# Two products per token row, one core: 25-token tiles with split stores become 15-token tiles with one store each

## The chip, the core and the metric

The kernel runs on one core of one Trainium2 chip. The metric is the device time of one execution in microseconds (us); lower is better. Before the change it is 239.96 us, the median of three runs (239.96 to 240.86). One further execution was recorded by the profiler: it took 239.6 us, of which 237.8 us lie between its first and its last instruction (the span). A difference of about 0.5%, 1.2 us, is the least that a measurement of this kernel can tell from no change.

## What is computed

```python
def reference(x, expert_indices, expert_weights):
    batch, seq, hidden = x.shape            # 16, 1024, 512
    k = expert_indices.shape[-1]            # 2
    x_expanded = x[:, :, np.newaxis, :].repeat(k, axis=2)
    weights = expert_weights[..., np.newaxis]
    return (x_expanded * weights).astype(np.float32)
```

There are 16,384 tokens of 512 numbers in fp32. Every token row is multiplied by its two weights, and both products are written. The indices are not used. So 33.6 MB of x and 0.13 MB of weights are read, 67.1 MB are written, and there are 16.8 million multiplications: hardly any arithmetic for the bytes.

## The kernel before, in words

The 16,384 tokens stand on 128 partitions, 128 tokens to a partition. They are cut into five tiles of 25 tokens per partition (L32) and a rest of 3 (`LAST`, L34, `z_tile`). One token of x is 2 KB on a partition, its two products are 4 KB, so that a tile is 50 KB in and 100 KB out on each partition. In a transfer of 128 partitions each of the 16 DMA engines moves 8 rows; a row is one contiguous piece and shows in the profile as one packet.

**Loads** (`load`, L67 to L85) are issued by ScalarE's queue (ACT). Tile 0 comes in two parts of 9 and 16 tokens (`FIRST`, L35), each later tile in one. Two tiles of x fit (`bufs=2`, L43), so `load(i + 2)` stands behind the work on tile i (L159) and must wait until that work has read the buffer. The loads of tiles 0 and 1 and of `z_tile` stand at the beginning.

**Weights** (`weights`, L92 to L105) are three transfers on SyncE's queue (SP), issued between the two parts of load 0: 25 KB for tile 0, 100 KB for tiles 1 to 4, 3 KB for the rest. Their rows are 200 bytes and 24 bytes long.

**Products** go to `o_ring` (L47), one buffer as large as a whole tile's output. `emit` (L148) cuts a tile into pieces of 13 and 12 tokens (tiles 0 and 1) or 9, 8 and 8 (tiles 2 to 4, L157). In each piece `fill` (L141) gives about two thirds of the tokens to VectorE (DVE) as tensor-by-tensor products of up to 4 tokens (L126, 128x4096 numbers out), with x and the weights broadcast, and the rest to ScalarE (ACT) as one ACTIVATE per token and weight (L116, 128x512).

**Stores** are issued by SP, one after each piece (L152): rows of 52, 48, 36, 32 or 12 KB, 14 stores in all. The same place of the ring is written again one tile later, and the engines wait for the store that still reads it. SP's queue (q1 in the profile) carries the weights and the stores; ACT's queue (q10) carries the loads of x.

Of the kernel before, what the change touches and what calls it, by code (L numbers as in the profile page):

```python
# [1 line left out]

# [4 lines left out]


@with_exitstack
def kernel(  # L10
    ctx: ExitStack,
    tc: tile.TileContext,
    x: bass.AP,
    expert_indices: bass.AP,
    expert_weights: bass.AP,
    out: bass.AP,
):
    nc = tc.nc

    batch, seq, hidden = x.shape  # L20
    k = expert_weights.shape[-1]
    P = nc.NUM_PARTITIONS
    ntok = batch * seq
    assert ntok % P == 0
    A_TOTAL = ntok // P

    f32 = mybir.dt.float32
    row = k * hidden
    CH = 4


    groups = [25, 25, 25, 25, 25]  # L32
    TX = max(groups)
    LAST = 3  # L34
    FIRST = [9, 16]  # L35
    assert sum(groups) + LAST == A_TOTAL

    xf = x.rearrange("b s h -> (b s) h")
    of = out.rearrange("b s k h -> (b s) (k h)")
    wf = expert_weights.rearrange("b s k -> (b s) k")  # L40

    w_pool = ctx.enter_context(tc.tile_pool(name="w_pool", bufs=1))
    x_pool = ctx.enter_context(tc.tile_pool(name="x_pool", bufs=2))  # L43
    o_pool = ctx.enter_context(tc.tile_pool(name="o_pool", bufs=1))

    w_tile = w_pool.tile([P, A_TOTAL * k], f32)
    o_ring = o_pool.tile([P, TX * row], f32)  # L47

    def rows(of_all, done, T):
        return of_all[done * P : (done + T) * P, :].rearrange(  # L50
            "(p a) n -> p (a n)", a=T
        )


    if LAST:
        z_pool = ctx.enter_context(tc.tile_pool(name="z_pool", bufs=1))
        z_tile = z_pool.tile([P, LAST * hidden], f32)

    tiles = []
    done = 0  # L60
    for n in groups:
        tiles.append((done, n))
        done += n

    loaded = []

    def load(i):  # L67
        if i >= len(tiles):
            return
        done, n = tiles[i]  # L70
        x_tile = x_pool.tile([P, TX * hidden], f32)
        src = rows(xf, done, n)
        steps = FIRST if i == 0 else [n]
        for e, step in enumerate(steps):
            at = sum(steps[:e])
            nc.scalar.dma_start(
                out=x_tile[:, at * hidden : (at + step) * hidden],
                in_=src[:, at * hidden : (at + step) * hidden],
            )
            if i == 0 and e == 0:  # L80
                for g in range(3):
                    weights(g)
        if i == 0 and LAST:
            nc.scalar.dma_start(out=z_tile, in_=rows(xf, A_TOTAL - LAST, LAST))
        loaded.append(x_tile)  # L85


    T0 = groups[0]
    G = len([n for n in groups[1:] if n == T0])
    head = (1 + G) * T0  # L90

    def weights(e):  # L92
        if e == 0:
            nc.sync.dma_start(out=w_tile[:, : T0 * k], in_=rows(wf, 0, T0))
        elif e == 1:
            nc.sync.dma_start(
                out=w_tile[:, T0 * k : head * k].rearrange("p (g n) -> p g n", g=G),
                in_=wf[T0 * P : head * P, :].rearrange(
                    "(g p a) n -> p g (a n)", g=G, p=P
                ),  # L100
            )
        else:
            nc.sync.dma_start(
                out=w_tile[:, head * k :], in_=rows(wf, head, A_TOTAL - head)
            )  # L105

    def product(engine, o_tile, t, x_in, c, m):

        o = t * row
        if engine is not None:  # L110
            for e in range(m * k):
                out_e = o_tile[:, o + e * hidden : o + (e + 1) * hidden]
                in_e = x_in[:, e // k * hidden : (e // k + 1) * hidden]
                w_e = w_tile[:, c + e : c + e + 1]
                if engine is nc.scalar or engine is nc.any and (c + e) % 3 == 2:
                    nc.scalar.mul(out=out_e, in_=in_e, mul=w_e)  # L116
                else:
                    nc.vector.tensor_scalar(
                        out=out_e,
                        in0=in_e,  # L120
                        scalar1=w_e,
                        scalar2=None,
                        op0=mybir.AluOpType.mult,
                    )
            return
        nc.vector.tensor_tensor(  # L126
            out=o_tile[:, o : o + m * row].rearrange(
                "p (t k h) -> p t k h", t=m, k=k
            ),
            in0=x_in[:, : m * hidden]  # L130
            .rearrange("p (t h) -> p t h", t=m)
            .unsqueeze(2)
            .to_broadcast([P, m, k, hidden]),
            in1=w_tile[:, c : c + m * k]
            .rearrange("p (t k) -> p t k", t=m)
            .unsqueeze(3)
            .to_broadcast([P, m, k, hidden]),
            op=mybir.AluOpType.mult,
        )

    def fill(o_tile, x_in, c, m):  # L141
        v = m - m // 3
        for t in range(0, v, CH):
            u = min(t + CH, v)
            product(None, o_tile, t, x_in[:, t * hidden : u * hidden], c + t * k, u - t)
        product(nc.scalar, o_tile, v, x_in[:, v * hidden :], c + v * k, m - v)

    def emit(src, dst, c, cuts):  # L148
        for at, to in zip(cuts, cuts[1:]):
            o_tile = o_ring[:, at * row : to * row]  # L150
            fill(o_tile, src[:, at * hidden : to * hidden], c + at * k, to - at)
            nc.sync.dma_start(out=dst[:, at * row : to * row], in_=o_tile)  # L152

    for i in range(2):
        load(i)
    for i, (done, n) in enumerate(tiles):
        cuts = [0, 13, n] if i < 2 else [0, 9, 17, n]  # L157
        emit(loaded[i], rows(of, done, n), done * k, cuts)
        load(i + 2)  # L159
    emit(  # L160
        z_tile,
        rows(of, A_TOTAL - LAST, LAST),
        (A_TOTAL - LAST) * k,
        [0, LAST],
    )

# [1 line left out]
_INS = ['x', 'expert_indices', 'expert_weights']  # L168
_OUTS = [((16, 1024, 2, 512), 'float32')]


# [23 lines left out]
```

## Time and profile before

| what | value |
|---|---|
| median of three runs | 239.96 us |
| profiled execution, its own time | 239.6 us |
| its span | 237.8 us |
| DVE busy | 99.1 us |
| ACT busy | 49.1 us |
| moved by DMA | 100.80 MB in 3841 packets |

The profile is one execution. "Busy" is the time in which an engine executes something; the DMA line of the page gives, for 40 equal slices, the mean busy share of the 16 DMA engines in tenths. For each DMA queue the page gives the packets, the bytes and the time that the packets took as a share of the time of 16 engines; the same three numbers can be asked for any window of the span. "To landing" is the time from the issue of a transfer until its completion is signalled.

### The profile page before, as it was taken

Reading aid. Unit: us, or ns where it says so; the run is one execution under the profiler, and the core shown is the slowest. Engines: PE = TensorE matmul, PEld = TensorE weight load, DVE = VectorE, ACT = ScalarE, POOL = GpSimd, SP = SyncE. Lnnn points to the kernel's source line nnn. Section 1 sums busy time; section 2 is a strip of 40 time slices with the busy share of each in tenths; the row PEclk is TensorE's granted clock in tenths of the full one; section 3 lists DMA queues with packets and bytes.
Section 4 is the critical chain, followed back from the end, with each engine's and each line's share of the span. In section 5 each row is a group of like instructions: output and inputs, shape, how many; then the busy total and the mean of one; then the engine's idle time right before and its main releaser. Section 6 shows DMA issues by size and latency. Waiting matters only on the chain.

```text
span 237.8 us, 214 instructions
## 1 busy us (share of the span) xinstructions
DVE 99.1 (42%) x29; ACT 49.1 (21%) x77; POOL 0.2 (0%) x4
## 2 busy tenths in 40 slices
DVE  0599600000069292089005964008292946823000
ACT  0008900000062160060005260004040540402000
POOL 0000000000000000000000000000000000000000
DMA  7999999999999999999999999999999999999996
GB/s 255 447 411 465 476 441 413 414 425 430 430 397 397 488 430 454 424 430 406 404 444 432 453 402 453 441 408 457 440 409 441 419 424 443 459 404 441 441 441 265
DMA packets 3841, 100.80 MB, mean 424 GB/s; under 512 B 1152, under 2 KB 1152, under 8 KB 1280
## 3 DMA queue, kind: packets, MB, share of 16 engines
q1 hardware_dynamic: 2832, 67.24, 65.7%
q10 hardware_dynamic: 1008, 33.55, 33.2%
q14 instruction: 1, 0.01, 0.0%
HBM read 33.69 MB, written 67.11 MB: 424 GB/s over the span
## 4 chain that ended last, share of the span: by engine, by line
DMA 68%; DVE 20%; issue 2%; ACT 1%; DVEq 0%; SPq 0%
DMA out_dram<-o_ring 65%; DVE o_ring L126 20%; DMA x_tile<-in_x_dram 3%; ACT o_ring L116 1%; DVEq L126 0%; SPq L152 0%
## 5 line engine op out<-in xcount | busy, mean ns | idle before, releaser
L126 DVE TENSOR_TENSOR o_ring<-x_tile,w_tile 128x4096 f32<-128x4096 f32 (+2 forms) x28 | 96.8, 3507 | 113.0 <-DMA out_dram<-o_ring 99.9
L116 ACT ACTIVATE o_ring<-x_tile,w_tile 128x512 f32<-128x512 f32 x74 | 46.5, 708 | 139.2 <-DMA out_dram<-o_ring 130.8
L116 ACT ACT_TABLE_LOAD x1 | 1.3, 1283 | 18.8 <-DMA x_tile<-in_x_dram 18.8
L126 DVE TENSOR_TENSOR o_ring<-z_tile,w_tile 128x2048 f32<-128x2048 f32 x1 | 2.3, 2292 | 4.3 <-DMA out_dram<-o_ring 4.3
L116 ACT ACTIVATE o_ring<-z_tile,w_tile 128x512 f32<-128x512 f32 x2 | 1.3, 713 | 8.3 <-DMA out_dram<-o_ring 8.3
L179 POOL MEMSET const-bfloat16-1.0<- 128x1 bf16 x1 | 0.1, 101 | 0.0
L179 POOL MEMSET const-uint8-127<- 128x1 uint8 x1 | 0.1, 101 | 0.0
L179 POOL MEMSET const-float32-0.0<- 128x1 f32 x1 | 0.1, 98 | 0.2 <-issue 0.2
L179 POOL MEMSET const-float32-1.0<- 128x1 f32 x1 | 0.1, 98 | 0.0
## 6 DMA issues: line engine op xcount, KB each, us to landing
x_tile<-in_x_dram ACTq DMA_DIRECT2D x4, 6400.0 KB, 31.5
out_dram<-o_ring SPq DMA_DIRECT2D x6, 4096.0 KB, 24.4
out_dram<-o_ring SPq DMA_DIRECT2D x3, 4608.0 KB, 30.0
out_dram<-o_ring SPq DMA_DIRECT2D x2, 6656.0 KB, 33.2
out_dram<-o_ring SPq DMA_DIRECT2D x2, 6144.0 KB, 44.3
x_tile<-in_x_dram ACTq DMA_DIRECT2D x1, 4096.0 KB, 17.6
x_tile<-in_x_dram ACTq DMA_DIRECT2D x1, 2304.0 KB, 8.1
out_dram<-o_ring SPq DMA_DIRECT2D x1, 1536.0 KB, 20.5
```

The costliest lines, as they stand in the source:

```text
L116: nc.scalar.mul(out=out_e, in_=in_e, mul=w_e)
L126: nc.vector.tensor_tensor(out=o_tile[:, o : o + m * row].rearrange("p (t k h) -> p t k h", t=m, k=k), in0=x_in[:, : m * hidden] .rearrange ...
L179: nc = _bacc.Bacc("TRN2", target_bir_lowering=False, num_devices=1)
```

## The change

The tiles become eight of 15 tokens and a rest of 8. x tiles are 30 KB on a partition (two of them), and the output is no longer a ring but two buffers of a whole tile, 60 KB each. Each tile has one store, of 60 KB rows; the rest has one of 32 KB rows.

All products become single ones of 128x512: in a full tile the first 18 of the 30 are `tensor_scalar` on DVE, the other 12 are ACTIVATEs on ACT (`cut = round(m * k * 0.6)`); in the rest it is 10 and 6.

The weights move from SP's queue to ACT's, in five transfers instead of three: those of tile 0 behind the first part of load 0 (7 tokens), those of tiles 1 and 2, 3 and 4, and 5 to 7 behind its second part (8 tokens), then those of the rest. Load 1 follows, and the load of `z_tile` (8 tokens) after it. Their rows are 120 bytes, and 64 bytes for the rest.

```diff
-    groups = [25, 25, 25, 25, 25]
+    groups = [15] * 8
     TX = max(groups)
-    LAST = 3
-    FIRST = [9, 16]
+    LAST = 8
+    FIRST = [7, 8]
+    PARTS = [[(0, 1)], [(1, 3), (3, 5), (5, 8)]]
...
-    o_pool = ctx.enter_context(tc.tile_pool(name="o_pool", bufs=1))
+    o_pool = ctx.enter_context(tc.tile_pool(name="o_pool", bufs=2))
...
-            if i == 0 and e == 0:
-                for g in range(3):
-                    weights(g)
-        if i == 0 and LAST:
-            nc.scalar.dma_start(out=z_tile, in_=rows(xf, A_TOTAL - LAST, LAST))
+            if i == 0:
+                for first, end in PARTS[e]:
+                    weights(first, end)
...
+    def weights(first, end):
+        G = end - first
+        nc.scalar.dma_start(
+            out=w_tile[:, first * TX * k : end * TX * k].rearrange(
+                "p (g n) -> p g n", g=G
             ),
+            in_=wf[first * TX * P : end * TX * P, :].rearrange(
+                "(g p a) n -> p g (a n)", g=G, p=P
+            ),
         )
...
     def fill(o_tile, x_in, c, m):
+        cut = round(m * k * 0.6)
+        for e in range(m * k):
+            out_e = o_tile[:, e * hidden : (e + 1) * hidden]
+            in_e = x_in[:, e // k * hidden : (e // k + 1) * hidden]
+            w_e = w_tile[:, c + e : c + e + 1]
+            if e < cut:
+                nc.vector.tensor_scalar(
+                    out=out_e,
+                    in0=in_e,
+                    scalar1=w_e,
+                    scalar2=None,
+                    op0=mybir.AluOpType.mult,
+                )
+            else:
+                nc.scalar.mul(out=out_e, in_=in_e, mul=w_e)
...
+    def emit(x_in, dst, c, n):
+        o_tile = o_pool.tile([P, TX * row], f32)
+        fill(o_tile, x_in, c, n)
+        nc.sync.dma_start(out=dst, in_=o_tile[:, : n * row])
...
+    load(0)
+    nc.scalar.dma_start(
+        out=w_tile[:, (A_TOTAL - LAST) * k :], in_=rows(wf, A_TOTAL - LAST, LAST)
+    )
+    load(1)
+    nc.scalar.dma_start(out=z_tile, in_=rows(xf, A_TOTAL - LAST, LAST))
     for i, (done, n) in enumerate(tiles):
-        cuts = [0, 13, n] if i < 2 else [0, 9, 17, n]
-        emit(loaded[i], rows(of, done, n), done * k, cuts)
+        emit(loaded[i], rows(of, done, n), done * k, n)
         load(i + 2)
     emit(
+        z_tile, rows(of, A_TOTAL - LAST, LAST), (A_TOTAL - LAST) * k, LAST
     )
```

More of the change, by code (lines that the diff above doesn't have):

```diff
@@ L28 @@
     row = k * hidden
-    CH = 4
-    groups = [25, 25, 25, 25, 25]
+    groups = [15] * 8
     TX = max(groups)
-    LAST = 3
-    FIRST = [9, 16]
+    LAST = 8
+    FIRST = [7, 8]
+    PARTS = [[(0, 1)], [(1, 3), (3, 5), (5, 8)]]
     assert sum(groups) + LAST == A_TOTAL
@@ L43 @@
     x_pool = ctx.enter_context(tc.tile_pool(name="x_pool", bufs=2))
-    o_pool = ctx.enter_context(tc.tile_pool(name="o_pool", bufs=1))
+    o_pool = ctx.enter_context(tc.tile_pool(name="o_pool", bufs=2))
     w_tile = w_pool.tile([P, A_TOTAL * k], f32)
-    o_ring = o_pool.tile([P, TX * row], f32)
     def rows(of_all, done, T):
@@ L52, in rows @@
         )
-    if LAST:
-        z_pool = ctx.enter_context(tc.tile_pool(name="z_pool", bufs=1))
-        z_tile = z_pool.tile([P, LAST * hidden], f32)
+    z_pool = ctx.enter_context(tc.tile_pool(name="z_pool", bufs=1))
+    z_tile = z_pool.tile([P, LAST * hidden], f32)
     tiles = []
@@ L79, in load @@
             )
-            if i == 0 and e == 0:
-                for g in range(3):
-                    weights(g)
-        if i == 0 and LAST:
-            nc.scalar.dma_start(out=z_tile, in_=rows(xf, A_TOTAL - LAST, LAST))
-        loaded.append(x_tile)
[L88 to L128, printed above, removed]
-            ),
[L130 to L138, printed above, removed]
@@ L139, in product @@
+            if i == 0:
+                for first, end in PARTS[e]:
+                    weights(first, end)
+        loaded.append(x_tile)
+    def weights(first, end):
[3 more added lines that the diff above has]
+                "p (g n) -> p g n", g=G
+            ),
+            in_=wf[first * TX * P : end * TX * P, :].rearrange(
+                "(g p a) n -> p g (a n)", g=G, p=P
+            ),
         )
     def fill(o_tile, x_in, c, m):
-        v = m - m // 3
@@ L143, in fill @@
[L143 to L152, printed above, removed]
@@ L154 @@
-    for i in range(2):
-        load(i)
+        cut = round(m * k * 0.6)
[13 more added lines that the diff above has]
+                nc.scalar.mul(out=out_e, in_=in_e, mul=w_e)
@@ L159 @@
         load(i + 2)
     emit(
[L161 to L164, printed above, removed]
+        z_tile, rows(of, A_TOTAL - LAST, LAST), (A_TOTAL - LAST) * k, LAST
     )
```

## The prediction

> **What bounds the kernel now.** I read the page from the top: span, engines, slices, queues, chain.
>
> ```profile
> span 237.8 us, 214 instructions
> DVE 99.1 (42%) x29; ACT 49.1 (21%) x77; POOL 0.2 (0%) x4
> DMA  7999999999999999999999999999999999999996
> DMA packets 3841, 100.80 MB, mean 424 GB/s; under 512 B 1152, under 2 KB 1152, under 8 KB 1280
> q1 hardware_dynamic: 2832, 67.24, 65.7%
> q10 hardware_dynamic: 1008, 33.55, 33.2%
> DMA 68%; DVE 20%; issue 2%; ACT 1%; DVEq 0%; SPq 0%
> ```
>
> DVE works 42% of the span and ACT 21%; the 16 DMA engines are at 90% or more in every slice but the first and the last. The two queues' packets fill 65.7 + 33.2 = 98.9% of 16 engines' span, 235.2 us of each engine. The chain names DVE for 20%, but the slices show that DMA moved other pieces beside that work. How much is not DMA? Three windows:
>
> ```profile
> 0.00:3.00 3.00, 0.00 (x0) 0.00 (x0) 0.20 (x4) 1.00 0.44 104
> 232.00:235.00 3.00, 0.00 (x0) 0.00 (x0) 0.00 (x0) 1.00 0.87 369
> 235.00:237.80 2.80, 0.00 (x0) 0.00 (x0) 0.00 (x0) 1.00 0.39 167
> ```
>
> The column before the last is the DMA share. The first window lacks 0.56 x 3 = 1.7 us: the first packet starts near 1.7, about 1.0 after its issue at 0.7. The last two lack 0.4 and 1.7 us: the end of the queue, the last signal and the closing instructions. The rest is a full DMA queue. Bytes stay the same, so the change can win only in time per packet, or lose where the queue runs empty.
>
> **Time per packet.** Windows that hold one size each: 55 to 60 (52 KB stores), 170 to 180 (32 KB stores), 25 to 30 (50 KB loads on q10 beside weights on q1).
>
> ```profile
> q1 hardware_dynamic: 39, 2.08, 95.8%
> ```
> ```profile
> q1 hardware_dynamic: 132, 4.20, 97.3%
> ```
> ```profile
> q10 hardware_dynamic: 48, 2.46, 113.9%
> q1 hardware_dynamic: 48, 0.01, 1.0%
> ```
>
> A 52 KB packet takes 0.958 x 5 us x 16 / 39 = 1.965 us. 4.20 MB are 128 packets of 32 KB (the 4 others are markers): 0.973 x 10 x 16 / 128 = 1.216 us. So 20 KB more cost 0.749 us, 0.0375 per KB, and a packet has 0.018 us of its own. That gives 1.891 for 50 KB; the third window has 1.139 x 5 x 16 / 48 = 1.898, so loads follow the same line. A weight packet took 0.010 x 5 x 16 / 48 = 0.0167 us.
>
> **The sum, for one DMA engine** (8 packets of each transfer). Before: stores 16 x 1.965 (52 KB) + 16 x 1.816 (48) + 24 x 1.366 (36) + 48 x 1.216 (32) + 8 x 0.467 (12) = 31.4 + 29.1 + 32.8 + 58.4 + 3.7; loads 8 x 0.692 (18 KB) + 8 x 1.216 (32) + 32 x 1.891 (50) + 8 x 0.243 (6) = 5.5 + 9.7 + 60.5 + 1.9. Together 233.0, and 48 weight packets 0.8: 233.8, against the 235.2 of the page. The missing 1.4 are slow packets and markers; one place shows them, the window 45 to 50, in which the last load ahead of the stores ends:
>
> ```profile
> q10 hardware_dynamic: 33, 1.69, 88.8%
> ```
>
> 0.888 x 5 x 16 / 33 = 2.15 us each, 0.26 too long, x 33 / 16 = 0.5 us of each engine.
>
> After: 64 x 2.265 (60 KB) + 8 x 1.216 (the 32 KB store) + 56 x 1.142 (30 KB) + 8 x 0.542 (14) + 16 x 0.617 (16, second part and z) = 145.0 + 9.7 + 64.0 + 4.3 + 9.9 = 232.9, and 72 weight packets 1.2: 234.1. Fewer large packets save 0.1, 24 more small ones cost 0.4: **+0.3 us**. I leave the slow packets at their 1.4; they could be anything from 0 to about twice that, since their cause is where transfers begin and end and both kernels have such places. A 60 KB packet is longer than any in the trace. If rows came as two packets, 64 x 0.018 = 1.2 us would be added.
>
> **Does the queue ever run empty?** The order of the two queues decides. Windows 40 to 45 and 93 to 95, the second with a load issued at 91.04:
>
> ```profile
> q10 hardware_dynamic: 47, 2.41, 111.5%
> q1 hardware_dynamic: 47, 0.00, 0.5%
> ```
> ```profile
> q1 hardware_dynamic: 12, 0.64, 73.8%
> q10 hardware_dynamic: 4, 0.20, 23.6%
> ```
> ```profile
> x_tile<-in_x_dram ACTq DMA_DIRECT2D x1, 6400.0 KB, 34.6
> ```
> ```profile
> 25.12 42.48 DMA out_dram<-o_ring
> ```
> ```profile
> w_tile<-in_expert_weights_dram SPq DMA_DIRECT2D x1, 3.0 KB, 50.4
> ```
>
> 47 against 47: an engine takes one packet from each queue in turn, whatever its size. So each tiny weight packet let a 50 KB load pass, the last 3 KB of weights needed 50.4 us, and the first store, issued at 25.12 behind them, landed 42.48 later. Taking the weights out of SP's queue ends that blockade. It is worth nothing by itself: q10 kept the engines busy meanwhile (the slices are all 9). What comes early is a store, and what is late in its place is a load. A load issued at 91.04 first appears around 94; 8 turns of 1.891 + 1.816 are 29.7, so that it is through at 123.7, and it was signalled at 125.6: about 1.9 us later, because the slowest engine counts. For x's first parts the same lag was smaller (below).
>
> Now the schedule after. Compute first:
>
> ```profile
> 0.72 0.89 ACTq L76 DMA_DIRECT2D x_tile<-in_x_dram  x2
> 18.79 1.28 ACT L116 ACT_TABLE_LOAD   x1 [18.79 <-DMA x_tile<-in_x_dram]
> 20.08 9.91 ACT L116 ACTIVATE o_ring<-x_tile,w_tile 128x512 f32<-128x512 f32 x16
> ```
> ```profile
> L126 DVE TENSOR_TENSOR o_ring<-x_tile,w_tile 128x4096 f32<-128x4096 f32 x17 | 74.9, 4423 | 98.1 <-DMA out_dram<-o_ring 84.9 <-DMA x_tile<-in_x_dram 8.9 <-issue 4.2
> L126 DVE TENSOR_TENSOR o_ring<-x_tile,w_tile 128x1024 f32<-128x1024 f32 x2 | 2.4, 1217 | 0.0
> ```
>
> ACT: 9.91 / 16 = 0.62 us apart, 12 in a tile 7.4 us. DVE's `tensor_scalar` is in no row. The two rows give (4423 - 1217) / 3072 = 1.044 ns per number and 148 ns fixed. At that rate 512 numbers take 0.68 us and 18 of them 12.3; with half the cost per number, because one tensor is streamed instead of two, 0.415 and 7.5. I take the lower end, by the operands, and keep 12.3 for a rival. The Trainium skill, "VectorE: DVE Perf Modes", section "The perf-mode tier table (the rule you actually need)", has fp32 `tensor_scalar` at twice the rate of `tensor_tensor`: 1227 against 2293 ns for 2048 numbers (the tensor-by-tensor row of that size here has 2285, no row has the other). By its figures I estimate 0.43 us for 512, and the fill would be 7.7 us.
>
> Start: 50 KB of x before were through at about 1.7 + 5.5 + 9.7 + 0.5 = 17.4 by the sum and seen at 18.79, lag 1.2 to 1.4 us. After: first part through at 6.5, second at 11.5 (weights of tile 0 between them, 0.1), seen at 12.7; table load 1.28 and 12 ACTIVATEs end at 21.4. Store 0 and load 2 are issued at 21.4, first packets about 1.0 later. Weights (64 packets, 1.1), load 1 and z keep q10 busy until 21.6 and 26.5. No gap, 4 us to spare.
>
> From 22.4 stores alternate with z's last 7 packets: 7 x (2.265 + 0.617) = 20.2, to 42.6; store 0's eighth beside load 2's first, 3.4, to 46.0. Load 2's other seven beside store 1: 7 x 3.4 = 23.8, to 69.8. Load 2 is seen at 71.0 (lag 1.2) to 71.7 (1.9). Until then nobody can fill tile 2: buffer 0 has been free since 47. Store 1 ends at 73.2, and load 3's last seven packets (8.0) end at **81.2**: there all issued work is done. Fill 2 ends at 71.0 + 7.5 = 78.5, issue to packet 1.0: **79.5**. 1.7 us to spare, 1.0 with the larger lag; I cost 0.1 for engines that run ahead. This is the one thin place. ACT waits in fill 2 for x, and load 4 stands behind it on ACT's queue, store 2 behind it on SP's, so both queues would dry up together. Later, store 2 and load 4 take 8 x 3.4 = 27.3 us, and at the end a store alone takes 8 x 2.265 = 18.1, against 1.9 + 7.5 + 1.0 = 10.4 for lag, fill and issue; even 12.3 gives 15.2. Two output buffers therefore suffice; DVE's and ACT's work lies beside transfers everywhere else. The end (last packets, signal) is unchanged.
>
> **Forecast:** 239.6 + 0.3 + 0.1 = 240.0 by the profiled execution. The median of the runs lies 0.36 above it, hence **240.4 us**, no measurable change.
>
> **Rivals.**
> - *The gap at 81 opens* (slower). It decides at lag + fill + issue = 81.2 - 69.8 = 11.4 us, that is at a fill of 9.2, 0.51 us per `tensor_scalar`. With 0.68 the gap is 71.0 + 12.3 + 1.0 - 81.2 = 3.1 us: 243.5; with the larger lag 3.8. For it: no row shows the operation, and the alternation is well shown. Against: the halved operand. By the skill's figure of the section above the gap stays shut. Chance 0.20 (with gaps from 0.9 up).
> - *The weights stall the load queue* (slower). Five small transfers now stand in one queue between loads, with nothing on the other queue to cover them until 22. At the row's 0.0167 each they cost 1.2 in all. If each of the two stretches drains the engines once, at the 1.0 us from issue to first packet, 1.9 is added: 242.3; with one drain for each transfer 4.8: 245.2. For it: in the trace small packets always stood beside a large one. Against: load follows load on q10 without a visible gap. Chance 0.14. The Trainium skill, "DMA: Bandwidth & Descriptors", section "Bandwidth", calls transfers under 64 KB descriptor-dominated and gives 0.95 us for 64 KB; four transfers of 15 to 45 KB and one of 8 KB would by that cost at most about 4.8 us, as an estimate. No row here shows small transfers alone.
> - *The handovers get cheaper* (faster). The 1.4 us of slow packets vanish because stores and loads alternate from 22 on: 239.0, and with up to 0.7 less at the uneven end 238.3. For it: the 0.5 us seen where weights and loads ended together. Chance 0.11.
> - *Rows are cut in two packets*, so that the one 60 KB row is not one: 1.2 more, 241.6, but loads pass sooner. Chance 0.02.
>
> The forecast keeps 0.53.
>
> **How the numbers follow.** A measurement of this kernel can tell about 0.5%, 1.2 us, from no change: 238.8 to 241.2. Faster: 0.11, of which I put a little back into "same" since 239.0 lies inside: 0.09. Slower: 0.20 + 0.14 + 0.02, all but their smallest gaps: 0.33. Same: 0.58. The range reaches down to 238.8, into the cheaper handovers, and up to 243.6, which takes in the gap at 0.68 and the two drains and leaves out the five.
>
> **What would show it.** Right: DMA slices all 9, queue shares that sum to about 235.5 us of each engine; 60 KB packets at 2.265 us; a `tensor_scalar` near 0.42; store 0 landing soon after 46 instead of at 67.6; load 2 landing near 71 and no DMA gap at 81. Wrong: a slice of 8 or less near 81 with DVE at 0.5 us or more; DMA share below 0.95 between 6 and 13; large packets off the line of 0.0375 us per KB, which would shift every term alike.

## The result and the profile after

The changed kernel takes 252.07 us (median of six runs, 250.9 to 253.03) against 240.2 us for the kernel before (median of six beside them): 1.0487 times the time, interval 1.0453 to 1.0521. It is slower by 11.9 us; 240.4 had been forecast, and 243.6 was the upper end of the range. The profiled execution has a span of 250.1 us, 12.3 us more than before.

The page of the changed kernel, in the order of the lines shown of before:

```profile
span 250.1 us, 366 instructions
DVE 61.8 (25%) x154; ACT 64.8 (26%) x103; POOL 0.2 (0%) x4
DMA  7999999899998999999999999999999988279977
DMA packets 3970, 100.81 MB, mean 403 GB/s; under 512 B 1536, under 2 KB 1536, under 8 KB 1536
q1 hardware_dynamic: 1296, 67.11, 63.4%
q10 hardware_dynamic: 2672, 33.69, 32.7%
```

The bytes are the same, and neither computing engine is busy for more than 26% of the span. Two things changed. The queues' packets took 96.1% of 250.1 us, 240.3 us of each engine, where 235.2 had been needed: **5.1 us more in the packets**. And 9.8 us of an engine hold no packet, where it had been 2.6: **7.2 us more without a packet**. Together that is the whole 12.3.

Packets first. The sum of the prediction gave 234.1 for this kernel, so slow packets and markers are 6.2 us instead of 1.4. A window late in the span, 222 to 232, has stores of tile 7 and of nothing else:

```profile
q1 hardware_dynamic: 64, 3.93, 91.0%
```

That is 0.910 x 10 x 16 / 64 = 2.275 us for a 60 KB packet, where 2.265 was computed: the length by itself costs nothing extra. Most of the slow ones stand in the long stretch before, 24 to 198, in which stores and loads take turns: of the 5.8 us of an engine by which single packets exceed the line (those over 0.15 us too long), 5.1 start in it.

Now the time without a packet. Windows of the changed kernel; the DMA share is the column before the last:

```profile
196.00:209.00 13.00, 0.00 (x0) 0.00 (x0) 0.00 (x0) 1.00 1.02 437
209.00:212.00 3.00, 0.00 (x0) 0.00 (x0) 0.00 (x0) 1.00 0.66 287
212.00:221.00 9.00, 7.21 (x18) 7.46 (x12) 0.00 (x0) 1.00 0.43 184
```

From 209 to 221 the 16 engines miss 0.34 x 3 + 0.57 x 9 = 6.2 us each; in the last 9 us of it DVE and ACT fill tile 7, before that they wait. The share of 0.43 is not a pause of all engines: some are busy and the others have nothing. What they wait for stands in the waits and the timeline of the changed kernel:

```profile
DVE o_tile L99 <- DMA x_tile<-in_x_dram: 154.3, 7, 35.2
DVE o_tile L99 <- DMA out_dram<-o_tile: 1.8, 1, 1.8
```
```profile
212.63 7.21 DVE L99 TENSOR_SCALAR o_tile<-x_tile,w_tile 128x512 f32<-128x512 f32 x18 [20.71 <-DMA x_tile<-in_x_dram]
```

Before, the fills had waited for stores; now all seven later fills wait for x. Fill 7 starts at 212.6. The 16 completion marks of that load in the trace show why: the first engine had its share of x of tile 7 at 192.2, the ninth at 194.9, the last at 212.4. For the first load the same marks lie within 0.6 us. **The engines have drifted apart by 20 us**, and a fill waits for the last one.

### The profile page after: what moved, and what is told of

It is laid out like the page before. It is cut to its first block, busy times and chain, and to the rows that moved or that the text cites. A ratio compares the mean times of both kernels' runs of the same rounds, so it can differ in the third digit from the quotient of the medians.

```text
span 250.1 us, 366 instructions
## 1 busy us (share of the span) xinstructions
DVE 61.8 (25%) x154; ACT 64.8 (26%) x103; POOL 0.2 (0%) x4
## 3 DMA queue, kind: packets, MB, share of 16 engines
q10 hardware_dynamic: 2672, 33.69, 32.7%
## 4 chain that ended last, share of the span: by engine, by line
DMA 66%; another core or an unknown queue 11%; ACT 8%; DVE 2%; ACTq 2%; issue 0%; DVEq 0%
DMA out_dram<-o_tile 42%; DMA x_tile<-in_x_dram 24%; ACT o_tile L107 8%; DVE o_tile L99 2%; ACTq L83 1%; ACTq L115 0%; ACTq L72 0%; DVEq L150 0%; DVEq L99 0%; ACTq L107 0%
## 5 line engine op out<-in xcount | busy, mean ns | idle before, releaser
L99 DVE TENSOR_SCALAR o_tile<-x_tile,w_tile 128x512 f32<-128x512 f32 x144 | 57.8, 479 | 162.1 <-DMA x_tile<-in_x_dram 154.3
L107 ACT ACTIVATE o_tile<-x_tile,w_tile 128x512 f32<-128x512 f32 x96 | 59.7, 709 | 146.2 <-DMA x_tile<-in_x_dram 146.2
L107 ACT ACT_TABLE_LOAD x1 | 1.3, 1283 | 12.7 <-DMA x_tile<-in_x_dram 12.7
L99 DVE TENSOR_SCALAR o_tile<-z_tile,w_tile 128x512 f32<-128x512 f32 x10 | 4.0, 479 | 1.8 <-DMA out_dram<-o_tile 1.8
L107 ACT ACTIVATE o_tile<-z_tile,w_tile 128x512 f32<-128x512 f32 x6 | 3.8, 708 | 1.7 <-DMA out_dram<-o_tile 1.7
## 6 DMA issues: line engine op xcount, KB each, us to landing
x_tile<-in_x_dram ACTq DMA_DIRECT2D x7, 3840.0 KB, 51.3
x_tile<-in_x_dram ACTq DMA_DIRECT2D x1, 2048.0 KB, 11.1
```

Source lines behind the costliest of these rows:

```text
L99: nc.vector.tensor_scalar(out=out_e, in0=in_e, scalar1=w_e, scalar2=None, op0=mybir.AluOpType.mult,)
```

## The experiments

Time in packets is the two queues' share times the span; the rest of the span is time without one. Both are means over the 16 engines, in us.

| kernel | median | ratio to before, interval | in packets | without |
|---|---|---|---|---|
| before | 240.2 | | 235.2 | 2.6 |
| changed | 252.07 | 1.0487, 1.0453 to 1.0521 | 240.3 | 9.8 |
| e1 one queue | 242.63 | 1.0099, 1.0071 to 1.0127 | 236.2 | 4.6 |
| e2 weights on SP | 245.18 | 1.0208, 1.0165 to 1.0251 | 235.7 | 7.3 |
| e3 two stores | 240.5 | 1.0033, 1.0006 to 1.006 | 235.7 | 2.9 |
| e4 before, weights on ACT | 240.52 | 1.0011, 0.9992 to 1.0029 | 235.3 | 3.3 |
| e5 rest earlier | 251.94 | 1.0489, 1.044 to 1.0538 | 239.4 | 11.0 |
| e6 two stores, issued late | 242.42 | 1.0099, 1.0071 to 1.0126 | 237.1 | 3.1 |
| e7 tiles of 12 | 253.83 | 1.0576, 1.0529 to 1.0622 | 240.6 | 11.6 |
| e8 before, single products | 239.93 | 1.0006, 0.9982 to 1.003 | 234.9 | 3.3 |
| e9 tiles of 12, three x tiles | 251.28 | 1.0465, 1.0443 to 1.0488 | 238.7 | 10.5 |
| e10 two stores, two loads | 251.27 (all four) | 1.0305, 1.0283 to 1.0328 | 239.9 | 13.4 |
| e11 free transfers | 248.39 | 1.0342, 1.0196 to 1.0488 | 236.7 | 11.4 |
| e12 free, two stores | 241.68 | 1.0062, 1.0022 to 1.0101 | 236.7 | 3.4 |

The four runs of e10 gave 247.4 and 247.5, and 255.0 and 255.3; its ratio goes by the first pair, and its profile, with the last two columns, is of the execution that took 255.0.

### e1: loads behind stores in one queue

```diff
-            nc.scalar.dma_start(
+            (nc.scalar if i < 2 else nc.sync).dma_start(
                 out=x_tile[:, at * hidden : (at + step) * hidden],
```

> The changed kernel with the loads of tiles 2 to 7 issued by SP, behind the store before them, so that nothing takes turns after the start. Theory (the loss of 12 us comes from the two queues taking turns: the engines drift apart, load 7 is through on the slowest engine at 212, fill 7 is late and the queue is dry from 211 to 221, 6.8 us; about 5.4 us more are slow packets that stand only where loads and stores alternate): both go, 239 to 241 us, load 7 lands a store ahead of need. Rival (60 KB packets are slow by themselves, or single products disturb the stores): the slow packets stay, 244 to 247 us. Rival (one queue leaves gaps because a load is behind a whole store): slower than the changed kernel.

Measured 242.63 us, 1.6 above what the theory gave. Its direction holds and its size nearly: without turns, 4.1 of the 5.1 us in the packets go, and there is no dry stretch. 60 KB packets are still there, so they are not slow by themselves. What remains is an uneven end; the last window of e1:

```profile
234.00:240.80 6.80, 0.00 (x0) 0.00 (x0) 0.00 (x0) 1.00 0.41 178
```

Of its 6.8 us, 4.0 lack a packet. In the kernel before the last 5.8 us have a share of 0.64, 2.1 us without.

### e2: weights back on SP's queue

```diff
     def weights(first, end):
-        nc.scalar.dma_start(
+        nc.sync.dma_start(
```

The transfer of the rest's weights is changed in the same way.

> The changed kernel with the five weight transfers back on SP's queue. Theory: the loads of the start are through at 27 us either way and the weights let store 0 begin at about that time, so almost nothing moves: 250 to 253 us. Rival (weights in the load queue cost by themselves, or a blocked store 0 is what the kernel before lived on): 240 to 246 us.

Measured 245.18 us: a miss of the theory, which had expected no difference. Putting the weights back takes 6.9 of the 11.9 us away. The DMA issues of two windows, 20 to 24 (store 0 and load 2) and 28 to 32 (load 3), first of the changed kernel, then of e2, show what they do; the last column is the time to landing. Store 1, which the changed kernel issues in the second window too, is left out.

```profile
out_dram<-o_tile SPq DMA_DIRECT2D x1, 7680.0 KB, 32.7
x_tile<-in_x_dram ACTq DMA_DIRECT2D x1, 3840.0 KB, 42.2
...
x_tile<-in_x_dram ACTq DMA_DIRECT2D x1, 3840.0 KB, 65.2
```
```profile
out_dram<-o_tile SPq DMA_DIRECT2D x1, 7680.0 KB, 42.4
x_tile<-in_x_dram ACTq DMA_DIRECT2D x1, 3840.0 KB, 18.6
...
x_tile<-in_x_dram ACTq DMA_DIRECT2D x1, 3840.0 KB, 37.5
```

With the weights ahead of it on SP's queue store 0 is held back (42.4 instead of 32.7), and loads 2 and 3 pass: load 3 lands after 37.5 instead of 65.2 us. From then on fills wait for stores, as before the change. The blockade that the prediction had called worth nothing gave the loads a lead. The slow packets are almost gone: with markers they are 235.7 - 234.1 = 1.6 us. Yet stores and loads take turns here as they do in the changed kernel (439 packets of SP's queue and 419 of ACT's start between 104 and 186, where the changed kernel has 410 and 436). What differs in that stretch is that the fills wait for stores and not for loads. The engines still end unevenly, with 7.3 us of an engine without a packet: thirteen end within 235.8 to 236.3, three only at 241.2 to 241.8.

### e3: two stores for each tile

```diff
-        fill(o_tile, x_in, c, n)
-        nc.sync.dma_start(out=dst, in_=o_tile[:, : n * row])
+        half = [0, (n + 1) // 2, n]
+        for at, to in zip(half, half[1:]):
+            part = o_tile[:, at * row : to * row]
+            fill(part, x_in[:, at * hidden :], c + at * k, to - at)
+            nc.sync.dma_start(out=dst[:, at * row : to * row], in_=part)
```

> The changed kernel with each tile filled and stored in two parts of 8 and 7 tokens, rows of 32 and 28 KB. Theory (one packet from each queue in turn): a 30 KB load packet now alternates with about as much store instead of twice as much, the loads are through after half a tile of stores, load 7 is long there when fill 7 is due, and the dry stretch at the end goes: 243 to 246 us if the slow packets stay, 239 to 241 if they go too. Rival (the length of the row store plays no part; the smaller tiles do): 250 to 253 us.

Measured 240.5 us: nearly the whole loss is gone, and both halves of it. The loads of e3 and their waits:

```profile
x_tile<-in_x_dram ACTq DMA_DIRECT2D x7, 3840.0 KB, 23.2
```
```profile
DVE o_tile L99 <- DMA out_dram<-o_tile: 84.9, 5, 24.7
DVE o_tile L99 <- DMA x_tile<-in_x_dram: 38.1, 3, 25.3
```

The same seven loads landed after a median of 51.3 us in the changed kernel. A tile now brings 16 store packets for 8 load packets to an engine, the load is through after half of them, and only three fills wait for x.

### e4 and e8: the other parts alone, in the kernel before

e4 issues the three weight transfers of the kernel before on ACT's queue; the edit of the other two is the same:

```diff
-            nc.sync.dma_start(out=w_tile[:, : T0 * k], in_=rows(wf, 0, T0))
+            nc.scalar.dma_start(out=w_tile[:, : T0 * k], in_=rows(wf, 0, T0))
```

> The kernel before with its three weight transfers issued by ACT between the two parts of load 0, nothing else changed. Store 0 then starts at about 26 instead of 51 and alternates with load 1 and load 2. Theory (alternating is what costs): the stores and loads mix earlier and longer, 241 to 246 us, with more slow packets than the 1.3 us of an engine that the kernel before has. Rival (alternating 50 KB with 52 KB costs nothing): 239.5 to 240.5 us.

e8 gives the kernel before the single products:

```diff
-        v = m - m // 3
-        for t in range(0, v, CH):
-            u = min(t + CH, v)
-            product(None, o_tile, t, x_in[:, t * hidden : u * hidden], c + t * k, u - t)
+        v = m - round(m * 0.4)
+        product(nc.vector, o_tile, 0, x_in, c, v)
```

> The kernel before with its tensor-by-tensor products replaced by single products of 128x512, 60% on DVE and 40% on ACT, as the changed kernel has them; tiles, stores and weights as before. Theory: the fills become shorter, but DMA is full anyway: 239 to 241 us. Rival (the products disturb the transfers, or their earlier stores change the turns): over 242 us.

Measured 240.52 and 239.93 us; neither differs from the kernel before by more than the intervals. Products and weights are not the cause by themselves. In e4 the rival was right: store 0 alternates early there too, but 52 KB with 50 KB, and nothing is lost. So it is not alternation as such.

### e5: the rest stored earlier

```diff
     for i, (done, n) in enumerate(tiles):
+        if i == 6:
+            emit(
+                z_tile, rows(of, A_TOTAL - LAST, LAST), (A_TOTAL - LAST) * k, LAST
+            )
         emit(loaded[i], rows(of, done, n), done * k, n)
```

The call at the end is taken away.

> The changed kernel with the rest of 8 tokens filled and stored between tiles 5 and 6 instead of last. Its x has been there since 37, so a store of 9.7 us is added to what is queued while fills 6 and 7 wait for x. Theory (the dry stretch from 211 to 221, 6.8 us of an engine, stands there because x of tile 7 is late and nothing else is queued): it shrinks to 0 to 2 us, 245 to 247 us in all; the slow packets stay. Rival (the engines that run dry do so because they are simply faster, and the slowest engine sets the time): 250 to 252 us.

Measured 251.94 us, no gain. Windows of e5:

```profile
198.00:208.00 10.00, 7.22 (x18) 7.46 (x12) 0.00 (x0) 1.00 0.63 271
240.00:250.40 10.40, 0.00 (x0) 0.00 (x0) 0.00 (x0) 1.00 0.34 148
```

The stretch from 212 to 221 is covered (share 1.01), but 3.7 us are missing from 198 to 208 and 6.9 at the end. The theory that a late fill 7 costs 6.8 us by itself falls. The rival holds: engines that run dry are ahead of the others, and whatever is queued for them, the slowest engine sets the time.

### e6: the halves issued late

```diff
-        nc.sync.dma_start(out=dst, in_=o_tile[:, : n * row])
+        half = [0, (n + 1) // 2, n]
+        for at, to in zip(half, half[1:]):
+            nc.sync.dma_start(
+                out=dst[:, at * row : to * row], in_=o_tile[:, at * row : to * row]
+            )
```

> The changed kernel with each tile filled whole as it is, and then stored in two transfers of 32 and 28 KB rows issued one behind the other. Theory (the ratio of a load packet to a store packet decides): as with two fills and two stores, 240 to 242 us, since the loads gain a lead. Rival (what helped was that half a tile is issued while the other half is still being filled): 246 to 252 us.

Measured 242.42 us, just above what the theory gave: 9.7 of the 11.9 us go by cutting the store alone, with the fill as in the changed kernel. The earlier issue of e3 is worth another 1.9. The bytes lie at the same addresses as in the changed kernel, so where the rows lie in memory is not the cause by itself.

### e7: tiles of 12 tokens

```diff
-    groups = [15] * 8
+    groups = [12] * 10
...
-    FIRST = [7, 8]
-    PARTS = [[(0, 1)], [(1, 3), (3, 5), (5, 8)]]
+    FIRST = [5, 7]
+    PARTS = [[(0, 1)], [(1, 3), (3, 6), (6, 10)]]
```

> The changed kernel with ten tiles of 12 tokens: loads of 24 KB rows, one store of 48 KB rows each, the ratio of 1 to 2 kept, every packet shorter than the longest that the kernel before has without harm. Theory (turn-taking at 1 to 2 leaves the loads without a lead and lets the engines drift): slower again, 246 to 251 us, with slow packets of over 3 us of an engine. Rival (packets of 60 KB are the trouble): 240 to 242 us and slow packets of 1 to 2 us.

Measured 253.83 us, even above what the theory gave. Packets of 24 and 48 KB, shorter than the 50 and 52 KB that do no harm in the kernel before, lose as much as 30 and 60 KB do. The length is not the trouble.

### e9: three tiles of x

To e7, with its tiles of 12 tokens, a third tile of x is added:

```diff
-    x_pool = ctx.enter_context(tc.tile_pool(name="x_pool", bufs=2))
+    x_pool = ctx.enter_context(tc.tile_pool(name="x_pool", bufs=3))
...
     load(1)
+    load(2)
...
-        load(i + 2)
+        load(i + 3)
```

> The kernel with tiles of 12 tokens (253.8 us) with three tiles of x instead of two, so that the load of tile i + 3 stands behind the work on tile i and the loads start with a lead of a tile. Packets, their ratio of 1 to 2 and everything else stay. Theory A (x that is late lets the fills wait for the slowest engine's load; a lead ends that): 240 to 244 us and at most 2.5 us of slow packets for an engine. Theory B (a load queue that never empties lets the engines drift at 1 to 2, lead or not): 246 to 254 us, 4 us or more of slow packets.

Measured 251.28 us, 2.5 less than e7, inside theory B's range. With markers its slow packets are about 3.5 us by the prediction's way of adding up (238.7 - 235.2), a little under theory B's 4 and above theory A's 2.5. A lead given to the loads at the start does not last. From the timeline of e9, fill 2 still waits for a store, and a later one waits for x again:

```profile
44.23 5.63 DVE L99 TENSOR_SCALAR o_tile<-x_tile,w_tile 128x512 f32<-128x512 f32 x14 [19.51 <-DMA out_dram<-o_tile]
...
213.25 5.63 DVE L99 TENSOR_SCALAR o_tile<-x_tile,w_tile 128x512 f32<-128x512 f32 x14 [16.07 <-DMA x_tile<-in_x_dram]
```

### e10: two stores and two loads

To e3 the same cut of the loads is added:

```diff
-        steps = FIRST if i == 0 else [n]
+        steps = FIRST if i == 0 else [8, 7]
```

> The kernel with two stores for each tile (240.5 us) with the loads cut in the same way, rows of 16 and 14 KB, so that a load packet is again half of a store packet and a tile again needs as many load packets as store packets. Theory (the ratio of the packets decides, through the turns): the loads lose their lead again and the slow packets come back, 246 to 253 us. Rival (two stores help because they are issued and buffered in halves): it stays at 240 to 242 us.

Even in the shorter pair of runs the time is 247.5 us: most of the loss that two stores had removed is back. A load packet is again half a store packet, and a tile brings 16 of each. The halves issued early do not help any more, so the relation of the packets decides, not the number of stores. The DMA issues of the profiled execution, one of the longer pair, show that the second part of a tile lands after 51.3 us, as a whole tile does in the changed kernel; in e3 a whole tile needs 23.2:

```profile
x_tile<-in_x_dram ACTq DMA_DIRECT2D x8, 2048.0 KB, 37.1
x_tile<-in_x_dram ACTq DMA_DIRECT2D x8, 1792.0 KB, 51.3
```

### e11 and e12: the transfers without the coupling

```diff
-    o_pool = ctx.enter_context(tc.tile_pool(name="o_pool", bufs=2))
+    o_pool = ctx.enter_context(tc.tile_pool(name="o_pool", bufs=1))
...
+    o_tiles = [o_pool.tile([P, TX * row], f32, name=f'o_tile{j}') for j in range(2)]
+
-    def emit(x_in, dst, c, n):
-        o_tile = o_pool.tile([P, TX * row], f32)
-        fill(o_tile, x_in, c, n)
+    def emit(x_in, dst, c, n, o_of, fresh):
+        o_tile = o_tiles[o_of % 2]
+        if fresh:
+            fill(o_tile, x_in, c, n)
```

`fresh` is true for tiles 0 and 1 alone, so the products of all other tiles and of the rest are left out; e12 is the same edit of e3. The transfers are the same, but not their order: the store of the rest (in e12 its first half), which waits for tile 0's products alone, is issued first, at 14.3 us in e11 and at 11.3 in e12.

> The changed kernel without the products of tiles 2 to 7 and of the rest: their stores send the two output buffers as tiles 0 and 1 left them, and no store or fill waits for x any more; only a load waits for the load two before it. All transfers, their sizes and queues stay, so that the turn-taking of 30 KB loads and 60 KB stores stands alone. Theory A (equal numbers of unequal packets taking turns make slow packets and drift by themselves): 3 us or more of slow packets for an engine, stores landing over more than 5 us, 241 to 247 us. Theory B (the drift comes from the coupling: fills that wait for the slowest engine's load): at most 2 us of slow packets, 237 to 239 us.

> The same with two stores for each tile (32 and 28 KB): products of tiles 2 to 7 and of the rest left out, turn-taking of 30 KB loads with stores of about their size. Both theories: at most 2 us of slow packets, 236 to 239 us; over 241 would mean that long alternation harms at any ratio.

Measured 248.39 us (two runs, a wide interval) and 241.68 us. The last windows of e11, then of e12:

```profile
48.00:210.00 162.00, 0.00 (x0) 0.00 (x0) 0.00 (x0) 1.00 1.00 430
210.00:234.00 24.00, 0.00 (x0) 0.00 (x0) 0.00 (x0) 1.00 1.04 449
234.00:236.00 2.00, 0.00 (x0) 0.00 (x0) 0.00 (x0) 1.00 0.36 154
236.00:248.10 12.10, 0.00 (x0) 0.00 (x0) 0.00 (x0) 1.00 0.13 56
```
```profile
120.00:236.00 116.00, 0.00 (x0) 0.00 (x0) 0.00 (x0) 1.00 1.00 432
236.00:240.10 4.10, 0.00 (x0) 0.00 (x0) 0.00 (x0) 1.00 0.27 116
```

After tiles 0 and 1 nothing waits for a fill in e11, and still it ends like this: for the last 12 us the share is 0.13, two of 16 engines. Linking packets that follow each other without a pause into 16 chains shows the rest. Twelve chains end within 235.8 to 236.3, nine of them without a slow packet after 27. The other four end at 241.2, 241.2, 245.0 and 246.9. Every engine has the same bytes to move and none of the chains pauses, so the four can be late only by slow packets, and hold nearly all of them. The spread of a store's completion marks grows through the span, from 0.7 us at 27 to 11.1 at 229, and stops growing when the loads end. In e12 the last store's marks spread over 2.2 us. In packets e11's mean engine spent only 1.5 us more than before; the loss is that four engines bear it.

Of theory A the drift holds: it comes without any wait of a fill, and the marks spread over 11.1 us. The size does not quite: the median lies above its 241 to 247 (the two runs took 246.9 and 249.9), and the slow packets are 2.6 us by the sum (236.7 - 234.1), not 3 or more. The rival, coupling alone, falls.

But the coupling has its share. By the ratios 8.2 of the 11.9 us are lost without it, in two runs that lie 3 us apart. Of slow packets the changed kernel has 6.2 us, e11 only 2.6, and e2, in which the fills wait for stores, 1.6. So turn-taking alone is shown to make most of the lost time, but less than half of the slow packets. That the rest of them comes from fills that wait for the slowest engine's load is argued from these three runs and not tested by itself.

e12 is a miss too: 241.68 us is above the 236 to 239 that both theories gave and above 241, which was to mean that long alternation harms at any ratio. Part of it is the number of rows: 128 of 32 and 28 KB in place of 64 cost 1.1 us by the sum. Its slow packets are then 236.7 - 235.2 = 1.5 us, about what the kernel before has, but its engines end 2.2 us apart. Long alternation with stores of the load's size costs little, not nothing.

What was not tried: bytes out are twice the bytes in, so a load packet of half the length and equal numbers of packets for a tile always come together in this kernel. Which of the two is the condition stays open. So does why the lead of the loads lasts in e2 and not in e9, what a slow packet waits for, and why it is four engines in e11.

## Why the prediction was wrong

- **What bounds the kernel** was right: bytes and time per packet. So was the line of 0.0375 us per KB (2.275 measured for 60 KB, 2.265 computed), and its 30 KB, 14 KB and 16 KB terms (medians 1.138, 0.535 and 0.611 us; 1.142, 0.542 and 0.617 computed).
- **The slow packets are the term that failed.** "I leave the slow packets at their 1.4; they could be anything from 0 to about twice that": they are 6.2. They were put down to places where transfers begin and end. The runs show that they come with long turn-taking of half packets with whole ones (e1, e3 and e6 take it away, e7 keeps it with shorter rows, e10 brings it back), and that more than half of them appear only where the fills wait for x as well (2.6 us in e11, 1.6 in e2). No stretch of the trace before contained that: there loads of 50 KB met stores of 52 to 32 KB, and no load was under way from 51.5 to 94.8 and from 123.5 to 140.4. e3 and e4 alternate too and lose under 1 us, e12 1.5.
- **One engine stood for sixteen.** The whole sum was "for one DMA engine", and the lag of the slowest was taken as 1.2 to 1.9 us from the trace before. In the changed kernel it grows to 20 us. That is why 7.2 us without a packet appeared: e5 and e11 show that filling the queue, or taking the waits away, does not win them back.
- **"It is worth nothing by itself"** of the blocked first store was wrong in this setting: e2 gains 6.9 us with the blockade restored. In the kernel before it was right (e4: no difference).
- **The schedule** gave the right kind of place and the wrong one. Store 0 landed at 54.2 instead of 47, load 2 at 64.9 instead of 71.0, so the thin place at 81 was passed; but load 3 then took turns with store 2 and landed at 95.3 instead of about 82, and every later fill waited for x.
- **The weights rival** falls. (Its prices of 1.9 and 4.8 us are 0.1 and 0.2 below what two and five drains of 1.0 us add up to.) x of tile 0 was seen whole at 12.73 (12.7 computed), and the window from 2 to 24 of the changed kernel is full, weights and all:

```profile
q10 hardware_dynamic: 1719, 8.92, 99.3%
```

- **The products** were right: 18 `tensor_scalar` in 7.21 us, 0.40 apart, where 0.415 was taken.

```profile
L99 DVE TENSOR_SCALAR o_tile<-x_tile,w_tile 128x512 f32<-128x512 f32 x144 | 57.8, 479 | 162.1 <-DMA x_tile<-in_x_dram 154.3
```

The estimate of 0.43 from the Trainium skill ("VectorE: DVE Perf Modes", section "The perf-mode tier table (the rule you actually need)") lies between that distance and the 479 ns that one takes by itself.

- **The range** reached 3.2 us over the forecast because each rival was priced on an even set of engines. A cost that falls on the slowest engine alone was in none of them.

The Trainium skill, "DMA: Bandwidth & Descriptors", section "Issuing engines are not separate DMA queues", says that issuing from several engines only saves the time of issuing. Here the choice of queue moved 9.4 us (e1) and 6.9 us (e2) with the same bytes and sizes; the measurement decides.

## What to carry to other kernels

Where two queues share the DMA engines, count the packets that each brings per tile, for an engine served them one for one here (47 against 47 in one window before): cut the larger transfer so that the one whose data is waited for needs clearly fewer turns. Judge a full DMA queue by its slowest engine (the spread of completions, a share of 0.1 to 0.6 at the end), not by the mean share. An order that looks like an accident, such as tiny transfers that hold back the first store, may be what gives the loads their lead.

## What was not expected of the hardware

Four of the 16 DMA engines took nearly all the slow packets in e11 and finished 5 to 11 us after the other twelve, which ended within 0.5 us of each other. In e2 three finished 5 to 6 us after the other thirteen. In the kernel before all sixteen ended within 0.7 us. One 60 KB packet of the changed kernel took 3.67 us where the median is 2.27.
